# A hybrid decoder layer on one core: the passage from LayerNorm 1 to the seven-product FFN stage, with residual rows, evictions and statistics at other places in the queues

## The chip, the cores and the metric

The kernel runs on one core of a Trainium2 chip. The metric is the device time of one execution in microseconds (us). Engines are named as the profile names them: PE (matrix products) with PEld (its weight loads), DVE (vector), ACT (scalar activations), POOL, and SP, which issues most loads. Each engine takes its instructions in the order in which the program issues them, and waits at the first whose inputs, or whose output buffer, are not there yet.

## What is computed

One layer of a decoder for 512 prompt tokens and 32 sample tokens (8 sequences of 4), with model width 1024 and FFN width 2816, all in float32. Cut to the part around the change:

```
x = layer_norm(ALPHA * x + (1 + g1) * y, ln1_g, ln1_b)      # y: the merged branches times w_out
u = x * (1 + sc2) + sh2
h = (silu(u @ w_gate) * (u @ w_up)) @ w_down
x = layer_norm(ALPHA * x + (1 + g2) * h, ln2_g, ln2_b)
```

`sc2`, `sh2`, `g1`, `g2` come from a conditioning vector, one for the prompt and one for each sample sequence. Ahead of this lie one input projection, a causal convolution, dilated attention over prompt and caches, and their merge.

## The kernel before

**Halves and splits.** Activations lie transposed, with channels on the 128 partitions and the 544 tokens along the free axis, and are worked on in two halves of 272 tokens (`HC`), called half 0 and half 1. Every matrix operand is split into a high and a low part in a format that PE takes faster than full float32, and a product is three passes: high by high, high by low, low by high (lines 199, 200 and 202 in `mm_group`). A weight tile of 128 by 1024 is therefore split before use by `prep_to`: ACT casts it to the high part (line 133), DVE subtracts to get the low part (line 134). `w_next(look)` prepares up to `look` tiles ahead and returns the next one. There are four raw buffers (`wr`); a load into one is issued by SP (line 117) when the tile that lay in it has been split.

**Output projection and LayerNorm 1 (lines 977 to 1007).** For each half, eight output tiles m = 0 to 7 are computed (24 products each); DVE adds each into the residual `z` (line 991, in half 1 also 995 and 997), and `stats.feed(m)` collects LayerNorm statistics: a running sum `lns` on DVE (line 881) and a running sum of squares `lnq` (the square on ACT, line 873, the addition on POOL, line 882). After each tile `tick()` advances the background generators in `bg` by one step. When a half is done, `ln1_gen` is put in `bg` and advanced once: `stats.finish` adds the last tile (line 918) and yields. The next step has PE add up the sums over partitions (lines 922 and 923, against a matrix of ones), ACT and DVE make the reciprocal deviation (926 to 935), and the normalised rows are turned into the FFN input `u2[h]`: DVE multiplies (954), ACT scales and shifts (956) and casts to the high part (960), DVE subtracts to the low part (950). For half 0 this is spread over the steps by `LN1_CUTS`, and after one empty step four further steps of two rows each make two things for each row k on ACT: a copy of the FFN input in `TF` (line 974), which is needed later, and the residual row `z * ALPHA * g + ALPHA * b` in place (line 975), which nothing reads before the down projection. The steps that are still left when half 1 is done are run in `while bg: tick()`, ahead of the last addition of half 1.

**First FFN tiles (j = 0, lines 1223 to 1300).** `w_gu` holds gate and up tiles in turn, here called gu0, gu1, and so on; tiles 2f and 2f+1 belong to hidden tile f. Hidden tiles 0 and 1 (gu0 to gu3) are computed for half 0 first (`first`), with the statistics of half 1 between its second and third group on PE, and then for half 1 (`second`, lines 1259 to 1265, 96 products). Hidden tiles 2 and 3 are classical: gate product `pg` (48 products), up product `pu` (48), then `gu_evict`: two sigmoids on ACT (1015), the gate multiplied in and the up product multiplied in on DVE (1017, 1019), cast and low part of the result (1021, 1023). The products lie in four PSUM banks of the pool `pmm`, so `pg` of hidden tile 3 takes the banks of `pg` of hidden tile 2 and cannot start before these have been read. The sigmoid tiles `sgf` come from two buffers (tag `w`).

Between these products the operands of the next stage are made: sums and differences of the blocks of u2 (`tf`, `t3`, `t4`, lines 1252 to 1257), and their high and low parts S1, S2, S3 and A22 (1253, 1256, 1269, 1272, 1275, 1278, 1279, 1289). `keep(k)` does for half 1 what line 975 does for half 0. `add_up` (POOL, line 1071) makes sums of the raw blocks of the weights into `SS`, whose buffer is that of `t3`; `unit` splits such a block (ACT 1087, DVE 1098).

**Seven-product stage (`seven`, hidden tiles 4 to 20).** A hidden tile takes seven products of half size (lines 1114 to 1116) in place of eight. The order of the work on all engines is written out by hand: while PE works at tile f, ACT, DVE and POOL split and add up the blocks of tile f + 1, and what is left of tile f's eviction (`rest`: `c12`, `lo0`, `m1`, `hi1`, `lo1`) runs at the start of the next tile. For j = 0 the tiles are 4, 5, 6 and 7; `copies` after each issues copies of the caches from ACT's queue.

**What sets the order.** PE, ACT, DVE and POOL run exactly in program order. A buffer that is taken again waits for the last reader of the tile that lay in it.

Of the kernel before, what the change touches and what calls it, by code (L numbers as in the profile page):

```python
# [9 lines left out]
AF = mybir.ActivationFunctionType  # L10
# [6 lines left out]
NT = 544  # L17
# [37 lines left out]
def hybrid_step_kernel(ctx: ExitStack, tc: tile.TileContext, I, O):  # L55
# [37 lines left out]
    def big_tile(i, shape, dt, name):  # L93
        return big.tile(shape, dt, tag=f"L{i}", name=name)
# [45 lines left out]
    def w_next(look=PLOOK):  # L140
        i = pos["use"]
        prep_to(i + look)
        pos["use"] = i + 1
        return preps.pop(i)
# [718 lines left out]
    class Stats:  # L863
# [42 lines left out]

        def finish(self, tail, pairs=(0, 2)):
            if tail:
# [8 lines left out]
            else:  # L917
                self.add(7)
                yield
                pq = ps_t.tile([128, 512], F32, tag="t", name="lnps2")  # L920
                pd = ps_o.tile([128, 512], F32, tag="o", name="lnps")
# [18 lines left out]
    def f32(ap):  # L940
        return ap.bitcast(F32)

    def ln1_gen(h, stats):
        sd = yield from stats.finish(False, (0, 2) if h else ())
        A = big_tile(5 + h, [128, 2, 8, HC], F32R, f"u2{h}")
# [22 lines left out]
        if h == 0:  # L968
            yield
            for k in range(8):  # L970
                if k % 2 == 0:
                    yield
                zk = stats.zt(k)
                act.activation(out=TF[0][:, k // 4, k % 4], in_=zk, func=AF.Identity, scale=G9[:, k, 0:1], bias=B9[:, k, 0:1])
                act.activation(out=zk, in_=zk, func=AF.Identity, scale=agb[:, 0, k:k + 1], bias=agb[:, 1, k:k + 1])

# [32 lines left out]

    def gu_evict(pg, pu, Hs, fi):  # L1010
        hs = list(pg)
        sg = {}
        for h in hs:
            sg[h] = tmp.tile([128, HC], F32, tag="w", name="sgf")
            act.activation(out=sg[h], in_=pg[h][:, :HC], func=AF.Sigmoid)
        for h in hs:
            dve.tensor_tensor(out=sg[h], in0=sg[h], in1=pg[h][:, :HC], op=ALU.mult)  # L1017
        for h in hs:
            dve.tensor_tensor(out=sg[h], in0=sg[h], in1=pu[h][:, :HC], op=ALU.mult)
        for h in hs:  # L1020
            act.copy(out=Hs[h][:, 0, fi], in_=sg[h])
        for h in hs:
            dve.tensor_tensor(out=Hs[h][:, 1, fi], in0=sg[h], in1=Hs[h][:, 0, fi].bitcast(F32), op=ALU.subtract)

    def down_evict(ps, m, h):
# [81 lines left out]
    def unit(f, n):  # L1107
        unit_high(f, n)()
# [110 lines left out]
    for j, (k0, k1) in enumerate(FF_CHUNKS):  # L1219
# [3 lines left out]
        if j == 0:  # L1223
# [21 lines left out]

            def keep(k):
                zk = z[:, k, HC:NT]
                act.activation(out=zk, in_=zk, func=AF.Identity, scale=agb[:, 0, k:k + 1], bias=agb[:, 1, k:k + 1])

# [6 lines left out]
            act.copy(out=T["S2"][:, 0], in_=tf[:, 3])  # L1256
            dve.tensor_tensor(out=t4, in0=tf[:, 1], in1=tf[:, 3], op=ALU.subtract)
            A = u2[1]
            for k in range(8):
# [7 lines left out]
            for i in range(2):  # L1267
                gu_evict({1: second[2 * i]}, {1: second[2 * i + 1]}, H, i)
            dve.tensor_tensor(out=T["S1"][:, 1], in0=tf[:, 0], in1=f32(T["S1"][:, 0]), op=ALU.subtract)
            prep_to(pos["use"] + 2)  # L1270
            pu = mm_group(w_next(2), u2, 8)
            dve.tensor_tensor(out=T["S2"][:, 1], in0=tf[:, 3], in1=f32(T["S2"][:, 0]), op=ALU.subtract)
            TA = big_tile(0, [128, 2, 2, 4, HC], F32R, "ta")
            T["S3"], T["A22"] = TA[:, 0], TA[:, 1]
            act.copy(out=T["S3"][:, 0], in_=t3)
            keep(0)
            keep(1)
            dve.tensor_tensor(out=T["S3"][:, 1], in0=t3, in1=f32(T["S3"][:, 0]), op=ALU.subtract)
            act.copy(out=T["A22"][:, 0], in_=t4)
            keep(2)  # L1280
            keep(3)
            own["SS"] = one.tile([128, 3, 4, 128], F32, tag="vT", name="ss")
            gu_evict(pg, pu, H, 2)
            prep_to(pos["use"] + 2)
            f = 4
            for n in ("S1", "S2", "S3"):
                add_up(f, n)
            pg = mm_group(w_next(2), u2, 8)
            dve.tensor_tensor(out=T["A22"][:, 1], in0=t4, in1=f32(T["A22"][:, 0]), op=ALU.subtract)
            own["S4"] = one.tile([128, 2, 4, 128], F32R, tag="osb", name="s4")  # L1290
            for k in range(4, 8):
                keep(k)
            unit(f, "A11")
            unit(f, "S1")
            add_up(f, "S4")
            pu = mm_group(w_next(1), u2, 8)
            unit(f, "S2")
            gu_evict(pg, pu, H, 3)
            unit(f, "A12")
            rest["a22"] = unit_high(f, "A22")  # L1300
        for f in wg:
            hooks = {}
            if f == wg[-1]:
                u = pos["use"] + 2
                hooks = {2: lambda: prep_to(u + 1), 4: lambda: prep_to(u + 2)}
            seven(f, f - k0, H, f + 1 in wg, hooks)
            copies(0.8)
        ring.clear()
# [181 lines left out]
```

## Time and profile before

| | us |
|---|---|
| median of 3 runs | 1039.72 (1038.31 to 1041.39) |
| the profiled execution | 1039.63 |
| its span in the profile | 1037.9 |
| PE busy | 989.9 (95%) |
| DVE busy | 647.1 (62%) |
| ACT busy | 480.8 (46%) |
| POOL busy | 233.5 (23%) |

Times in the rows of the profile are us from the start of the span. A row of the timeline gives the start, the duration, the engine, the line of the kernel, the operation, output and inputs by the program's names with the shape, and the count if equal neighbours were merged (the start is then the first one's). A bracket at the end gives the idle time of the engine just before, and what released it. Matmuls are pipelined, so that one starts about 0.125 us after the other although each is shown with 0.29 us. A row of the table of windows gives, for each engine, busy time and number of instructions, then the clock that PE was granted (1.00 is full), then the share and the rate of the DMA engines.

### The profile page before, as it was taken

How to read it: one execution, taken by the hardware profiler on the slowest of the kernel's cores; microseconds unless marked ns; L12 is line 12 of the kernel's file. 1: busy time of each engine (PE TensorE's matmuls, PEld its weight loads, DVE VectorE, ACT ScalarE, POOL GpSimd, SP SyncE). 2: the span in 40 equal slices, each digit the busy share in tenths (PEclk: the TensorE clock that was granted, in tenths of full speed). 3: DMA queues.
4: the chain of work that ended last, by engine and by line, in shares of the span. 5: the costliest groups of instructions: out<-in, count | busy, mean ns of one | idle time of the engine just before them, and what ended most of it. 6: DMA issues, size and time to landing. Idle time of an engine off the chain costs nothing.

```text
span 1037.9 us, 21539 instructions
## 1 busy us (share of the span) xinstructions
PE 989.9 (95%) x8964; PEld 946.5 (91%) x8964; DVE 647.1 (62%) x1156; ACT 480.8 (46%) x931; POOL 233.5 (23%) x279
## 2 busy tenths in 40 slices
PE   4999999999999999999999997889999999999995
PEld 3987999999989989999999987889999999999994
DVE  3422788879886554343228876757636885478687
ACT  3312235545447666543434356556315552266333
POOL 0201010010014310101103534034014440354046
PEclk9999999999999999999999998989999999999998
DMA  9898687686785574799943620124964668665612
GB/s 379 362 387 316 236 301 273 246 330 239 281 302 196 205 264 161 264 373 393 361 165 105 246 63 21 48 67 171 345 243 173 259 216 325 235 247 202 217 51 86
DMA packets 44945, 242.64 MB, mean 234 GB/s; under 512 B 7408, under 2 KB 10736, under 8 KB 37680
## 3 DMA queue, kind: packets, MB, share of 16 engines
q1 hardware_dynamic: 34592, 126.83, 34.0%
q10 hardware_dynamic: 7632, 88.43, 22.7%
q0 software_dynamic: 2624, 26.02, 6.2%
q8 instruction: 70, 1.15, 0.4%
q14 instruction: 27, 0.22, 0.1%
HBM read 231.36 MB, written 97.58 MB: 317 GB/s over the span
## 4 chain that ended last, share of the span: by engine, by line
PE 65%; DVE 11%; issue 8%; ACT 7%; POOL 5%; DMA 4%; ACTq 0%; DVEq 0%; POOLq 0%
PE mm L199 16%; PE mm L200 15%; PE mm L202 15%; POOL ss L1071 3%; DMA wr<-in_w_gu 2%; PE mm L1114 2%; PE mm L1115 2%; PE mm L1116 2%; PE od L740 2%; PE Sd L705 2%; PE adaps L334 1%; PE pt L516 1%; DVE mrg L829 1%; DMA wr<-in_w_in 1%; DVE wl L134 1%
## 5 line engine op out<-in xcount | busy, mean ns | idle before, releaser
L199 PE MATMUL mm<-u,wh 128*128 128x272 f32 x1016 | 285.0, 298 | 6.4 <-DVE sgf L1017 6.4
L200 PE MATMUL mm<-u,wh 128*128 128x272 f32 x1016 | 277.0, 290 | 0.0
L202 PE MATMUL mm<-u,wl 128*128 128x272 f32 x1016 | 213.7, 290 | 0.5 <-DVE wl L134 0.5
L199 PEld LDWEIGHTS mm<-u,wh 128*128 128x128 f32 x1016 | 193.7, 191 | 20.9 <-issue 11.0
L200 PEld LDWEIGHTS mm<-u,wh 128*128 128x128 f32 x1016 | 193.9, 191 | 0.4
L134 DVE TENSOR_TENSOR wl<-wr,wh 128x1024 fp32r<-128x1024 f32 (+2 forms) x100 | 116.3, 1164 | 85.8 <-ACT wh L133 85.0
L202 PEld LDWEIGHTS mm<-u,wl 128*128 128x128 f32 x1016 | 161.3, 190 | 0.7 <-DVE wl L134 0.7
L133 ACT CAST wh<-wr 128x1024 fp32r<-128x1024 f32 (+2 forms) x100 | 97.0, 972 | 66.5 <-PE mm L200 50.5
L439 DVE SCALAR_TENSOR_TENSOR convy<-glu,vec,convy 128x512 f32<-128x512 f32 x120 | 95.6, 796 | 2.5
L1071 POOL TENSOR_TENSOR ss<-wr 128x512 f32<-128x512 f32 x34 | 50.2, 1476 | 189.0 <-DVE s L1098 90.2
L200 PE MATMUL mm<-h,wh 128*128 128x272 f32 x240 | 64.7, 288 | 0.0
L199 PE MATMUL mm<-h,wh 128*128 128x272 f32 x240 | 64.5, 286 | 0.0
L1028 DVE SCALAR_TENSOR_TENSOR z<-mm,modT,z 128x272 f32<-128x272 f32 (+1 forms) x48 | 21.6, 478 | 51.2 <-PE mm L202 51.2
L637 ACT ACTIVATE qk<-mm,vec 128x272 f32<-128x272 f32 (+1 forms) x48 | 25.9, 627 | 56.5 <-PE mm L202 56.5
L202 PE MATMUL mm<-h,wl 128*128 128x272 f32 x240 | 49.6, 288 | 0.0
L1087 ACT CAST wh<-ss 128x512 fp32r<-128x512 f32 (+1 forms) x34 | 28.4, 835 | 43.6 <-POOL ss L1071 30.6
L199 PEld LDWEIGHTS mm<-h,wh 128*128 128x128 f32 x240 | 45.2, 188 | 0.0
L200 PEld LDWEIGHTS mm<-h,wh 128*128 128x128 f32 x240 | 45.1, 188 | 0.0
L509 ACT ACTIVATE P<-P,st 128x256 f32<-128x256 f32 x64 | 31.2, 489 | 28.3 <-DVE st L503 25.8
L654 POOL DMA_DIRECT2D out_kv<-qk x4 | 2.4, 599 | 182.5 <-ACT qk L637 182.5
L1114 PE MATMUL mm<-ta,wh 128*128 128x272 f32 x136 | 40.4, 297 | 0.9 <-DVE wg L1136 0.8
L200 PE MATMUL mm<-mrg,wo 128*128 128x272 f32 x128 | 37.9, 296 | 1.8 <-DVE mrg L829 1.7
(330 smaller groups left out, 2544.6 us busy)
## 6 DMA issues: line engine op xcount, KB each, us to landing
out_s<-in_c ACTq DMA_DIRECT2D x32, 2044.0 KB, 9.7
wr<-in_w_in SPq DMA_DIRECT2D x60, 512.0 KB, 6.5
wr<-in_w_gu SPq DMA_DIRECT2D x44, 512.0 KB, 4.1
KT<-in_kt SPq DMA_DIRECT2D x24, 792.0 KB, 8.0
VV<-in_vv SPq DMA_DIRECT2D x24, 768.0 KB, 7.4
gb<-in_w_ada POOLq DMA_DIRECT2D x8, 2048.0 KB, 16.6
out_s<-in_c ACTq DMA_DIRECT2D x8, 2032.0 KB, 10.5
ga<-in_w_ada SPq DMA_DIRECT2D x8, 1024.0 KB, 14.4
```

Of the source, the lines that this page charges most:

```text
L133: act.copy(out=hv, in_=raw)
L134: dve.tensor_tensor(out=lv, in0=raw, in1=hv.bitcast(F32), op=ALU.subtract)
L199: pe.matmul(ps[h][:, :HC], lhsT=hi[:, k], rhs=A[h][:, 0, k], start=(k == 0), stop=False)
L200: pe.matmul(ps[h][:, :HC], lhsT=hi[:, k], rhs=A[h][:, 1, k], start=False, stop=False)
L202: pe.matmul(ps[h][:, :HC], lhsT=lo[:, k], rhs=A[h][:, 0, k], start=False, stop=(k == nk - 1))
L439: dve.scalar_tensor_tensor(out=o, in0=src, scalar=sc, in1=o, op0=ALU.mult, op1=ALU.add)
L509: act.activation(out=p[:, a:b], in_=p[:, a:b], func=AF.Exp, bias=st[:, kd, s, hh, 0:1], accum_out=st[:, kd, s, hh, 1:2])
L637: act.activation(out=o, in_=src, func=AF.Identity, bias=V("b_in", col))
L1028: dve.scalar_tensor_tensor(out=zz[:, :n1], in0=ps[:, :n1], scalar=modT[:, 5, m, 0:1], in1=zz[:, :n1], op0=ALU.mult, op1=ALU.add)
L1071: pool.tensor_tensor(out=o, in0=x, in1=y, op=op)
L1087: act.copy(out=hi, in_=src_of(f, n))
L1114: pe.matmul(ps[:, :HC], lhsT=hi[:, k], rhs=B[:, 0, k], start=(first and k == 0), stop=False, skip_group_check=not first)
```

## The change

Three things are changed, none of which changes what is computed:

1. **LN1's first statistics one output tile later.** `finish` gets an argument `late`; for half 0 it yields a second time between the last addition and the products with `ones`. All later steps of half 0's `ln1_gen` thereby come one output tile of half 1 later.
2. **Residual rows put off.** Line 975 is gone from `ln1_gen`. `keep` now takes a count and works through 16 rows, half 0 first: four after the block differences, two after the low part of S2, two after the low part of A22, and two behind each of the four seven-product tiles of j = 0. Before, the eight rows of half 1 were four around S3 and A22 and four after the low part of A22.
3. **Classical evictions split in two.** `gu_evict` is divided into `gate_evict` (sigmoids and gate multiplication) and `up_evict` (the rest). For hidden tiles 2 and 3 the gate part is issued ahead of the up product's weights and products. With it the low parts of S1 and S2 move behind the issue of hidden tile 2's up product, S3 behind its eviction, the split of gu7 behind the three `add_up`, and in hidden tile 3 the blocks A11 and S1 of the weights ahead of the gate eviction, the high part of A22 and the S4 sum behind it.

```diff
-        def finish(self, tail, pairs=(0, 2)):
+        def finish(self, tail, pairs=(0, 2), late=False):
...
                 self.add(7)
                 yield
+                if late:
+                    yield
...
-        sd = yield from stats.finish(False, (0, 2) if h else ())
+        sd = yield from stats.finish(False, (0, 2) if h else (), h == 0)
...
-                act.activation(out=zk, in_=zk, func=AF.Identity, scale=agb[:, 0, k:k + 1], bias=agb[:, 1, k:k + 1])
...
+    def gate_evict(pg):
+        sg = {}
+        for h in pg:
+            sg[h] = tmp.tile([128, HC], F32, tag="w", name="sgf")
+            act.activation(out=sg[h], in_=pg[h][:, :HC], func=AF.Sigmoid)
+        for h in pg:
+            dve.tensor_tensor(out=sg[h], in0=sg[h], in1=pg[h][:, :HC], op=ALU.mult)
+        return sg
+
+    def up_evict(sg, pu, Hs, fi):
+        for h in sg:
+            dve.tensor_tensor(out=sg[h], in0=sg[h], in1=pu[h][:, :HC], op=ALU.mult)
+        for h in sg:
+            act.copy(out=Hs[h][:, 0, fi], in_=sg[h])
+        for h in sg:
+            dve.tensor_tensor(out=Hs[h][:, 1, fi], in0=sg[h], in1=Hs[h][:, 0, fi].bitcast(F32), op=ALU.subtract)
+
+    def gu_evict(pg, pu, Hs, fi):
+        up_evict(gate_evict(pg), pu, Hs, fi)
...
-            def keep(k):
-                zk = z[:, k, HC:NT]
-                act.activation(out=zk, in_=zk, func=AF.Identity, scale=agb[:, 0, k:k + 1], bias=agb[:, 1, k:k + 1])
+            keeps = [(k, h) for h in range(2) for k in range(8)]
+
+            def keep(n):
+                for _ in range(min(n, len(keeps))):
+                    k, h = keeps.pop(0)
+                    zk = z[:, k, h * HC:(h + 1) * HC]
+                    act.activation(out=zk, in_=zk, func=AF.Identity, scale=agb[:, 0, k:k + 1], bias=agb[:, 1, k:k + 1])
...
             dve.tensor_tensor(out=t4, in0=tf[:, 1], in1=tf[:, 3], op=ALU.subtract)
+            keep(4)
...
             pg = mm_group(w_next(2), u2, 8)
             for i in range(2):
                 gu_evict({1: second[2 * i]}, {1: second[2 * i + 1]}, H, i)
-            dve.tensor_tensor(out=T["S1"][:, 1], in0=tf[:, 0], in1=f32(T["S1"][:, 0]), op=ALU.subtract)
+            sg = gate_evict(pg)
             prep_to(pos["use"] + 2)
             pu = mm_group(w_next(2), u2, 8)
+            dve.tensor_tensor(out=T["S1"][:, 1], in0=tf[:, 0], in1=f32(T["S1"][:, 0]), op=ALU.subtract)
             dve.tensor_tensor(out=T["S2"][:, 1], in0=tf[:, 3], in1=f32(T["S2"][:, 0]), op=ALU.subtract)
+            keep(2)
+            up_evict(sg, pu, H, 2)
             TA = big_tile(0, [128, 2, 2, 4, HC], F32R, "ta")
             T["S3"], T["A22"] = TA[:, 0], TA[:, 1]
             act.copy(out=T["S3"][:, 0], in_=t3)
-            keep(0)
-            keep(1)
             dve.tensor_tensor(out=T["S3"][:, 1], in0=t3, in1=f32(T["S3"][:, 0]), op=ALU.subtract)
-            act.copy(out=T["A22"][:, 0], in_=t4)
-            keep(2)
-            keep(3)
             own["SS"] = one.tile([128, 3, 4, 128], F32, tag="vT", name="ss")
-            gu_evict(pg, pu, H, 2)
-            prep_to(pos["use"] + 2)
             f = 4
             for n in ("S1", "S2", "S3"):
                 add_up(f, n)
+            prep_to(pos["use"] + 2)
             pg = mm_group(w_next(2), u2, 8)
+            unit(f, "A11")
+            unit(f, "S1")
+            sg = gate_evict(pg)
+            act.copy(out=T["A22"][:, 0], in_=t4)
+            add_up(f, "S4")
             dve.tensor_tensor(out=T["A22"][:, 1], in0=t4, in1=f32(T["A22"][:, 0]), op=ALU.subtract)
             own["S4"] = one.tile([128, 2, 4, 128], F32R, tag="osb", name="s4")
-            for k in range(4, 8):
-                keep(k)
-            unit(f, "A11")
-            unit(f, "S1")
-            add_up(f, "S4")
+            keep(2)
             pu = mm_group(w_next(1), u2, 8)
             unit(f, "S2")
-            gu_evict(pg, pu, H, 3)
+            up_evict(sg, pu, H, 3)
...
             seven(f, f - k0, H, f + 1 in wg, hooks)
+            if j == 0:
+                keep(2)
             copies(0.8)
```

More of the change, by code (lines that the diff above doesn't have):

```diff
@@ L1007, in hybrid_step_kernel @@
         tick()
-    def gu_evict(pg, pu, Hs, fi):
-        hs = list(pg)
+    def gate_evict(pg):
         sg = {}
-        for h in hs:
+        for h in pg:
             sg[h] = tmp.tile([128, HC], F32, tag="w", name="sgf")
             act.activation(out=sg[h], in_=pg[h][:, :HC], func=AF.Sigmoid)
-        for h in hs:
+        for h in pg:
             dve.tensor_tensor(out=sg[h], in0=sg[h], in1=pg[h][:, :HC], op=ALU.mult)
-        for h in hs:
+        return sg
+    def up_evict(sg, pu, Hs, fi):
+        for h in sg:
             dve.tensor_tensor(out=sg[h], in0=sg[h], in1=pu[h][:, :HC], op=ALU.mult)
-        for h in hs:
+        for h in sg:
             act.copy(out=Hs[h][:, 0, fi], in_=sg[h])
-        for h in hs:
+        for h in sg:
             dve.tensor_tensor(out=Hs[h][:, 1, fi], in0=sg[h], in1=Hs[h][:, 0, fi].bitcast(F32), op=ALU.subtract)
+    def gu_evict(pg, pu, Hs, fi):
+        up_evict(gate_evict(pg), pu, Hs, fi)
     def down_evict(ps, m, h):
```

## Prediction

> **What bounds the kernel now.** I read the page first, its span and its busy shares.
>
> ```profile
> span 1037.9 us, 21539 instructions
> PE 989.9 (95%) x8964; PEld 946.5 (91%) x8964; DVE 647.1 (62%) x1156; ACT 480.8 (46%) x931; POOL 233.5 (23%) x279
> ```
>
> PE is the bound, and outside the stretch that is changed nothing moves. So what counts is where PE stands still between LN1 and the first seven-product tile: the timeline of PE alone, from 570 to 713 us, for its rows with a wait and for a few marks of place.
>
> ```profile
> 574.26 0.39 PE L200 MATMUL mm<-mrg,wo 128*128 128x272 f32 x1 [1.71 <-DVE mrg L829]
> ...
> 603.98 0.70 PE L922 MATMUL lnps<-lns,ones 128*128 128x272 f32 x2 [2.33 <-DVE lns L881]
> ...
> 638.86 1.28 PE L923 MATMUL lnps<-lnq,ones 128*128 128x272 f32 x2 [5.25 <-POOL lnq L882]
> ...
> 647.45 0.29 PE L1263 MATMUL mm<-u,wh 128*128 128x272 f32 x1
> ...
> 665.51 0.29 PE L199 MATMUL mm<-u,wh 128*128 128x272 f32 x1
> ...
> 666.64 0.52 PE L202 MATMUL mm<-u,wl 128*128 128x272 f32 x2 [0.47 <-DVE wl L134]
> ...
> 678.79 0.59 PE L199 MATMUL mm<-u,wh 128*128 128x272 f32 x1 [6.35 <-DVE sgf L1017]
> ...
> 693.34 0.29 PE L1114 MATMUL mm<-u,wh 128*128 128x272 f32 x1
> ...
> 712.25 0.39 PE L1114 MATMUL mm<-ta,wh 128*128 128x272 f32 x1 [0.24 <-DVE wg L1136]
> ```
>
> Four waits lie in the stretch: 2.33 + 5.25 + 0.47 + 6.35 = 14.4 us. Two of them cost more than their length, as the clock column of the windows shows:
>
> ```profile
> 575.00:576.00 1.00, 1.00 (x4) 1.00 (x5) 0.76 (x2) 0.17 (x1) 0.00 (x0) 0.50 0.98 386
> ...
> 604.00:610.00 6.00, 6.00 (x44) 5.84 (x45) 3.63 (x6) 2.49 (x4) 4.52 (x7) 1.00 0.35 110
> ...
> 643.00:644.00 1.00, 1.00 (x9) 1.00 (x8) 1.00 (x1) 0.00 (x0) 0.87 (x2) 0.89 0.04 16
> 684.00:685.00 1.00, 1.00 (x9) 1.00 (x9) 1.00 (x2) 0.24 (x1) 0.00 (x0) 0.91 0.83 311
> ```
>
> After the wait at 638.86 PE is back at full clock only about 643.2 (0.89 in its window), after that at 678.79 only about 684.2 (0.91). At half clock that loses 4.3/2 = 2.2 and 5.4/2 = 2.7 us. After the 2.33 us wait the clock stayed at 1.00, yet after one of 1.71 us (574.26) it fell to 0.50: what decides is not the length alone.
>
> **Part 1, LN1's sums.** The wait of 2.33 us goes: PE does tile 1 of half 1 first (24 products), and the last addition of half 0 is done by then. What comes late instead is read from DVE.
>
> ```profile
> 607.27 1.85 DVE L935 RECIPROCAL lnsd<-lnsd 128x272 f32<-128x272 f32 x1 [1.57 <-ACT lnsd L929]
> ...
> 612.67 0.46 DVE L991 SCALAR_TENSOR_TENSOR z<-mm,modT,z 128x240 f32<-128x240 f32 x1
> ...
> 613.91 0.79 DVE L954 TENSOR_TENSOR z<-z,lnsd 128x272 f32<-128x272 f32 x2
> ...
> 629.53 0.19 DVE L997 TENSOR_TENSOR z<-z,zsa 128x32 f32<-128x32 f32 x1
> ...
> 632.38 0.44 DVE L881 TENSOR_TENSOR lns<-lns,z 128x272 f32<-128x272 f32 x1
> ...
> 640.25 0.44 DVE L928 SCALAR_TENSOR_TENSOR lnsd<-lnps,lnsd 128x272 f32<-128x272 f32 x1 [0.15 <-PE lnps L923]
> ...
> 646.03 0.44 DVE L950 TENSOR_TENSOR u<-tf,u 128x272 fp32r<-128x272 f32 x1 [0.92 <-ACT u L960]
> ```
>
> DVE is nearly full here, so it and not PE paces half 1. Tile 1's residual and first sum (612.67 to 613.91, 1.24 us) now run before the reciprocal, in time that DVE spent waiting; the sums themselves come about 0.5 us later (PE ends tile 1 near 604.5, against 603.98). Net, the rest of DVE's row runs 0.7 us earlier: residual row 6 is ready at 629.72 - 0.7 = 629.0, the last addition at 632.1. A wait is added: half 1's first sum takes the buffer of half 0's and waits for PE's product; behind it stands only L928, which needs that product too, so I put it at zero (bounds 0 and 0.4). PE's full wait for a free bank, one tile later, I put at zero as well, since DVE paces.
>
> **Part 2, residual rows out of LN1.** The 5.25 us wait is for the squares of half 1, and its cause stands in ACT's row:
>
> ```profile
> 632.25 0.74 ACT L873 ACTIVATE lnsq<-z 128x272 f32<-128x272 f32 x2
> 632.89 0.60 ACT L974 ACTIVATE tf<-z,B,G 128x272 f32<-128x272 f32 x1
> ...
> 637.49 0.41 ACT L873 ACTIVATE lnsq<-z 128x272 f32<-128x272 f32 x1
> ```
>
> ```profile
> 638.04 0.76 POOL L882 TENSOR_TENSOR lnq<-lnq,lnsq 128x272 f32<-128x272 f32 x1 [3.64 <-ACT lnsq L873]
> ```
>
> Between the squares of rows 5, 6 and the last one stand eight instructions (four copies, four residual rows) in 4.6 us. After the change the residual rows are gone, but part 1 has pushed two more copies into this place, so six stand there. Independent rows take 0.53 us each (below, 2.13 for four). ACT is no longer behind, so it starts when row 6 is ready: 629.0 + 0.5 + 6 x 0.52 = 632.6 for the last square. POOL and PE follow 638.86 - 637.49 = 1.37 later: the product on the squares starts at 634.0, **4.9 us earlier**. PE, 2.3 earlier than before, still stands there for some 2.7 us in two pieces, for the sum and for the squares. Next on DVE's way to L928 stand gu3's cast and subtraction, queued behind the last square: 632.6 + 0.3 + 1.04 + 1.23 (durations of such a cast and subtraction below) = 635.2, against 640.25. So the chain of half 1 moves by 5.1 us, u2's first slice from 646.47 to 641.4.
>
> PE's second part starts with it, at 641.15 in place of 647.45 (its own work would let it start about 640.3 at full clock). From there 144 products to the up product of hidden tile 2 took 665.51 - 647.45 = 18.06, so it arrives at 659.2.
>
> **Part 3, four rows ahead of gu5.**
>
> ```profile
> 654.13 1.28 ACT L1015 ACT_TABLE_LOAD   x1
> ...
> 663.27 1.11 ACT L1256 CAST tb<-tf 128x1088 fp32r<-128x1088 f32 x1 [1.42 <-DVE tf L1255]
> 664.29 1.04 ACT L133 CAST wh<-wr 128x1024 fp32r<-128x1024 f32 x1
> ...
> 673.85 1.10 ACT L1275 CAST ta<-t 128x1088 fp32r<-128x1088 f32 x1 [3.15 <-DVE tb L1272]
> ...
> 676.87 1.12 ACT L1248 ACTIVATE z<-z,agb 128x272 f32<-128x272 f32 x2
> 677.88 0.66 ACT L1015 ACTIVATE sgf<-mm 128x272 f32<-128x272 f32 x2
> ...
> 681.08 2.13 ACT L1248 ACTIVATE z<-z,agb 128x272 f32<-128x272 f32 x4
> ```
>
> `keep(4)` stands right ahead of gu5's cast, with nothing to hide it: 664.29 - 5.1 + 2.1 = 661.3, done 662.3; the low part follows as before and PE's L202 stands at 666.64 - 5.1 + 2.1 = 663.6. So the wait of 0.47 grows to 3.1 for the high part plus 0.8 for the low part. Everything behind moves by only 3.0 us: the up product ends at 669.4, the evictions of `second` at 670.2 - 3.0 = 667.2.
>
> **Part 4, the split evictions.** The 6.35 us wait is for the gate multiplication of hidden tile 2, which stood behind S1, S2, S3, A22, four residual rows and the up product.
>
> ```profile
> 669.78 0.44 DVE L1023 TENSOR_TENSOR h<-sgf,h 128x272 fp32r<-128x272 f32 x1 [0.49 <-ACT h L1021]
> ...
> 674.98 1.29 DVE L1278 TENSOR_TENSOR ta<-t,ta 128x1088 fp32r<-128x1088 f32 x1 [1.22 <-ACT ta L1275]
> ...
> 681.21 1.23 DVE L134 TENSOR_TENSOR wl<-wr,wh 128x1024 fp32r<-128x1024 f32 x1 [0.35 <-ACT wh L133]
> ```
>
> Now it comes behind `second`. Its second sigmoid waits for the buffer freed at 667.2 (an added wait; queued behind it is gu6's cast); 0.4 and 0.5 later the bank is free, 668.2. gu6: cast 667.6 to 668.6, low part to 669.9. PE arrives at 669.3, so at most 0.2 is left of 6.35. Next is gu7, now behind more: S1 and S2 low (2 x 1.29) to 672.3, the up multiplications to 673.0, S3 high from 673.4, its low part to 675.8 (1.13 + 1.29 later, as at 673.85 and 674.98), then gu7's low part to 677.0. PE has done the gate product at 675.5 and the first four up products at 676.0, and waits 1.0 (bounds 0 and 2). The up product ends 5.8 later, 682.8, against 693.34: **10.5 us earlier**. The weight sums on POOL start at 675.9 and end near 681, before the stage needs them; the gate sigmoids, now waiting for PE ahead of A22, two rows and S2, find it done at 675.5.
>
> Against this stands the clock. A wait of 3.1 plus 0.8 within 4.4 us is between those that kept it and those that did not, and the 1.71 row says that it may well fall. Then the up product runs some 3.6 us at half clock and ends 1.8 later, but gu6 and gu7 are then no longer waited for (1.2), so 0.6 is left. I take it in. The Trainium skill, "TensorE: Matmul & The Clock Gate", has in its closing table that no idle gap above about 3 us should be left, and in Part 1 that the clock drops after one idle window of about 3.4 us. By it the waits of about 1 us cost nothing and this one stands at its edge; the row at 574.26 differs, it fell after 1.71. With no fall the sum would be 0.6 better.
>
> **Part 5, two rows behind each seven-product tile.** They stand on ACT ahead of the sigmoid of `c12` and of the split of S4.
>
> ```profile
> 706.09 0.40 ACT L1200 ACTIVATE wg<-c 128x272 f32<-128x272 f32 x1 [0.23 <-issue]
> ```
>
> ```profile
> 711.16 0.69 DVE L1098 TENSOR_TENSOR wl<-ss,hip 128x512 fp32r<-128x512 f32 x1 [1.09 <-POOL ss L1071]
> 711.76 0.43 DVE L1136 TENSOR_TENSOR wg<-wg,mm 128x272 f32<-128x272 f32 x1
> ```
>
> The split of S4 frees the buffer for POOL's next sum, whose split (711.16) stands on DVE ahead of U3 (711.76), and PE's product at 712.25 already waits 0.24 for U3. This loop has no slack: 1.05 us less the slack of 0.3 around L1200 (0.23 of it issue) is about 0.75 at PE in tile 5, and again in tile 6. Tile 7 has no next tile in this stage, tile 4 has nothing ahead of it: **1.5 us lost** (bounds 0 and 4 x 1.05 = 4.2).
>
> **Sum.** -10.5 + 0.6 + 1.5 = -8.4. The profiled execution took 1039.63, 1.7 beyond its span, and stands within 0.1 of the median, so 1039.7 - 8.4 = 1031.3 us.
>
> **Rivals.** *The four pairs are dearer*: if the loop does not catch up anywhere, they cost 4.2, and the sum is -5.7: 1034.0. For it speaks the 0.24 wait; against it that tile 7 lacks the split ahead of U3. *The pairs hide and the clock holds*: -10.5, 1029.2; for it speaks only that ACT is 46% busy. *The late sums gain nothing*: DVE ends half 1 where it did, the squares come 0.7 later and everything behind with them, 1032.0. *Slower, by table loads*: if the residual rows and the sigmoids do not share ACT's table, each of the seven places of `keep` costs two loads of 1.28 (654.13), 2.56 us. With six of them on the path and 1.5 of slack that is 13.9, and 1039.7 - 8.4 + 13.9 = 1045.2; it decides once loads stand at five places. Against it: the rows at 676.87 and 677.88 follow each other without one. *The change does not act*: if something else still stands in front of the gate multiplication, the 6.35 us stay with their cold clock, and only the 3.0 of part 3 less the 1.5 of part 5 is left: 1038.2. Against it: the two banks have no other reader.
>
> **Numbers.** The forecast 0.60, dearer pairs 0.15, hidden pairs 0.12, no gain from the late sums 0.07, table loads 0.03, no action 0.03. A measurement of this kernel tells a change from none beyond some 0.3%, 3.1 us. The first four are faster by more than that; no action mostly within it; so faster 0.93, same 0.03, slower 0.04. Range 1028.5 to 1034.5: from the hidden pairs, a little better, to the dear pairs.
>
> **What would show it.** Right: no wait for `lns` near 604; the product on the squares near 634; a wait of about 3 us at the up product of hidden tile 2, released by gu5 on ACT; less than 0.5 left at the next gate product; the first seven-product tile near 683; U3 waits of 0.7 to 1 us in tiles 5 and 6. Wrong: a table load between the rows, a wait above 2 us for gu7 or the weight sums, or a DVE that ends half 1 after 633.

## The result, and the profile after

The changed kernel took 1033.32 us, median of 4 runs (1032.24 to 1033.62); the kernel before, on the same chip, 1039.05, median of 4 (1038.31 to 1041.39). The ratio is 0.994, 95% interval 0.9927 to 0.9954: faster by 5.7 us, where 8.4 was forecast. The profiled execution took 1033.35 with a span of 1031.6, 6.3 less than before. Of all runs in this document one, the fourth of e7_no_pair_mid, was slow (1600.63 us at a granted clock of 0.557), and it is left out below.

The page of the kernel after: its span and busy time of each engine.

```profile
span 1031.6 us, 21539 instructions
PE 985.8 (96%) x8964; PEld 942.2 (91%) x8964; DVE 652.1 (63%) x1156; ACT 479.7 (47%) x931; POOL 236.3 (23%) x279
```

The work is the same to the instruction. But DVE became busier by 5.0 us and POOL by 2.8, with no instruction more: the same operations took longer. That is a first sign of the step that failed. It is a rough one: in a second profile of this kernel (e11_again, below) the rises are 2.6 and 1.7, and of the 5.0 here 3.4 belong to the four subtractions treated below.

The timeline of PE in the kernel after, from LN1 to the third seven-product tile: the rows that answer to those of before.

```profile
632.39 0.72 PE L924 MATMUL lnps<-lns,ones 128*128 128x272 f32 x2 [1.72 <-DVE lns L881]
634.65 1.27 PE L925 MATMUL lnps<-lnq,ones 128*128 128x272 f32 x2 [1.54 <-POOL lnq L882]
...
644.03 0.29 PE L1274 MATMUL mm<-u,wh 128*128 128x272 f32 x1
...
663.19 0.39 PE L199 MATMUL mm<-u,wh 128*128 128x272 f32 x1 [0.93 <-ACT wh L133]
...
664.45 0.52 PE L202 MATMUL mm<-u,wl 128*128 128x272 f32 x2 [0.49 <-DVE wl L134]
...
677.80 0.52 PE L202 MATMUL mm<-u,wl 128*128 128x272 f32 x2 [0.73 <-DVE wl L134]
...
683.41 0.29 PE L1120 MATMUL mm<-u,wh 128*128 128x272 f32 x1
...
693.33 0.39 PE L1120 MATMUL mm<-ta,wh 128*128 128x272 f32 x1 [2.18 <-DVE wg L1142]
...
705.06 0.39 PE L1120 MATMUL mm<-ta,wh 128*128 128x272 f32 x1 [0.88 <-DVE wg L1142]
...
716.80 0.39 PE L1120 MATMUL mm<-ta,wh 128*128 128x272 f32 x1 [0.90 <-DVE wg L1142]
```

Read it from the end. Tile 4 starts at 683.41, 9.9 us earlier than before (693.34). The 6.35 us wait at the gate product is gone; in its place 0.73 is left for gu7. From there on some of the gain is given back: 2.18 us in tile 4, where before listed no wait, 0.88 in tile 5 (0.24 before), and 0.90 in tile 6. So 9.9 - 2.2 - 0.6 - 0.9 = 6.2, against 6.3 between the spans. The gain was made as forecast, and lost in three waits for U3.

### The profile page after: what moved, and what is told of

It is laid out like the page before. It is cut to its first block, busy times and chain, and to the rows that moved or that the text cites. A ratio compares the mean times of both kernels' runs of the same rounds, so it can differ in the third digit from the quotient of the medians.

```text
span 1031.6 us, 21539 instructions
## 1 busy us (share of the span) xinstructions
PE 985.8 (96%) x8964; PEld 942.2 (91%) x8964; DVE 652.1 (63%) x1156; ACT 479.7 (47%) x931; POOL 236.3 (23%) x279
## 4 chain that ended last, share of the span: by engine, by line
PE 61%; DVE 12%; issue 8%; ACT 7%; POOL 6%; DMA 5%; ACTq 0%; DVEq 0%; POOLq 0%
PE mm L199 15%; PE mm L200 14%; PE mm L202 14%; POOL ss L1077 4%; DMA wr<-in_w_gu 3%; PE od L740 2%; PE mm L1120 2%; PE Sd L705 2%; PE mm L1121 2%; PE mm L1122 2%; PE adaps L334 1%; DVE mrg L829 1%; DMA wr<-in_w_in 1%; PE pt L516 1%; DVE wl L134 1%
## 5 line engine op out<-in xcount | busy, mean ns | idle before, releaser
L202 PE MATMUL mm<-u,wl 128*128 128x272 f32 x1016 | 213.2, 290 | 1.3 <-DVE wl L134 1.2
L202 PEld LDWEIGHTS mm<-u,wl 128*128 128x128 f32 x1016 | 160.4, 189 | 1.9 <-DVE wl L134 1.9
L202 PE MATMUL mm<-h,wl 128*128 128x272 f32 x240 | 49.6, 288 | 0.0
```

What stands on the lines that cost most here:

```text
L202: pe.matmul(ps[h][:, :HC], lhsT=lo[:, k], rhs=A[h][:, 0, k], start=False, stop=(k == nk - 1))
```

## The experiments

Each kernel is the changed kernel with the edit shown. The changed kernel itself was run once more with the last group, under the label e11_again, as a measure of what two sets of runs differ by:

> The changed kernel once more, beside the two runs that are built on it: 1033.3, as before, with a wait of 2.2 us for U3 in tile 4 and 0.9 in tiles 5 and 6. No theory expects anything else.

It took 1032.28 (1032.11 to 1033.26, 5 runs; ratio 0.9936, 0.9924 to 0.9949), 1.0 less than the first median. So a difference of 1 us between two kernels below tells nothing. PE's timeline of this execution, tiles 4 and 6 (tile 5 has no such wait):

```profile
692.28 0.39 PE L1120 MATMUL mm<-ta,wh 128*128 128x272 f32 x1 [2.18 <-DVE wg L1142]
...
715.77 0.40 PE L1120 MATMUL mm<-ta,wh 128*128 128x272 f32 x1 [0.52 <-DVE wg L1142]
```

The wait of tile 4 is as expected, those of tiles 5 and 6 are not (0 and 0.52 for 0.9 each). After tile 4's wait the granted clock fell to 0.50 here (window 694 to 697), where the first profile has 1.00, so PE came later to the next products and waited less. The time is the same: from the row of tile 4 to that of tile 6 it is 23.49 us here and 23.47 in the first profile. So waits of single products may be compared only between executions whose clock was the same there.

**First statistics put off: undone (e1_no_late).**

```diff
-        sd = yield from stats.finish(False, (0, 2) if h else (), h == 0)
+        sd = yield from stats.finish(False, (0, 2) if h else ())
```

> Part 1 undone alone: half 0's sums go back to one output tile earlier. Theory (DVE and ACT set when the product on the squares of half 1 can start, PE only waits there): PE stands 2.3 us near 604 again, but only four copies instead of six are left ahead of the last square, so that product starts near 633.8 in place of 634.65 and everything behind it is 0.5 to 0.9 us earlier than in the changed kernel: about 1032.5. PE's wait at the sums of half 1 is then under 1 us and its clock does not fall there. Rival (the 2.33 us were a gain of their own): the time goes up by 2.3 us, about 1035.6.

Measured: 1032.56 (1031.84 to 1034.22, 5 runs; ratio 0.9936, 0.9924 to 0.9949). Two rows of PE's timeline of this kernel:

```profile
603.87 0.70 PE L924 MATMUL lnps<-lns,ones 128*128 128x272 f32 x2 [2.33 <-DVE lns L881]
...
633.17 0.73 PE L924 MATMUL lnps<-lns,ones 128*128 128x272 f32 x2 [0.31 <-DVE lns L881]
```

The 2.33 us wait is back, and PE comes to the second sum that much later, so that it waits 0.31 there instead of 1.72, and not at all for the squares behind it. The wait only changes its place, since DVE and ACT pace half 1 of LN1. This part of the change is worth nothing that these runs can tell; the rival that it brings 2 us or more falls.

**Residual rows of half 0 back in LN1 (e2_rows_in_ln1).**

```diff
+                act.activation(out=zk, in_=zk, func=AF.Identity, scale=agb[:, 0, k:k + 1], bias=agb[:, 1, k:k + 1])
...
-            keeps = [(k, h) for h in range(2) for k in range(8)]
+            keeps = [(k, 1) for k in range(8)]
```

> Part 2 undone for half 0: its eight residual rows stand in LN1 again, so none is left behind the seven-product tiles; half 1's eight rows take the first places (four, two, two). Theory: twelve instructions in place of six ahead of the last square, so the product on the squares starts near 638.5, 3.9 us later, and the up product of hidden tile 2 and the first seven-product tile are later by as much; tiles 5 and 6 get back 1.5. Net 2.4 slower than the changed kernel, about 1035.7. Rival (PE's own work is the bound from there on, since its clock fell there anyway): first seven-product tile at most 1 us later and the time the same or better, 1032 to 1033.

Measured: 1035.8 (7 runs; ratio 0.9971, 0.996 to 0.9982), some 3 us slower than the changed kernel. PE's timeline of this kernel has the long wait for the squares again:

```profile
637.46 1.27 PE L925 MATMUL lnps<-lnq,ones 128*128 128x272 f32 x2 [5.41 <-POOL lnq L882]
```

The wait of tile 4 (at 696.13) stays at 2.18, to the hundredth. So it does not come from the eight rows moved here; those of half 1 are still in the passage and are treated below (e7, e4). Tiles 5 and 6 have no wait, but the clock fell to 0.58 ahead of them (697 to 700), so that this alone doesn't show what the rows cost there.

**Evictions whole, in the old order (e3_no_split).**

```diff
-            sg = gate_evict(pg)
+            dve.tensor_tensor(out=T["S1"][:, 1], in0=tf[:, 0], in1=f32(T["S1"][:, 0]), op=ALU.subtract)
...
-            keep(2)
-            up_evict(sg, pu, H, 2)
...
+            act.copy(out=T["A22"][:, 0], in_=t4)
...
+            gu_evict(pg, pu, H, 2)
+            prep_to(pos["use"] + 2)
...
-            up_evict(sg, pu, H, 3)
+            gu_evict(pg, pu, H, 3)
```

> Part 4 undone: from the gate product of hidden tile 2 on the order of the kernel before, the gate multiplication behind S1, S2, S3, A22 and the up product; rows where they are now (four ahead of gu5, two behind each of the four tiles), the other four after A22's low part. Theory: the wait for the bank comes back with some 5 us, the clock falls and loses 2 us more, but POOL's sums then run while DVE waits and tile 4 loses its 2.2 us wait. First seven-product tile 6 to 7 us later, net 4 slower: about 1037. Rival (parts 1 and 2 alone made the gain): within 1 us of the changed kernel.

Measured: 1036.02 (1035.02 to 1037.71, 11 runs; ratio 0.9968, 0.9959 to 0.9976). PE's timeline of this kernel:

```profile
676.08 0.44 PE L199 MATMUL mm<-u,wh 128*128 128x272 f32 x1 [4.34 <-DVE sgf L1017]
```

The gate product waits 4.34 us again, and the wait in tile 4 is gone: the four POOL sums take 1.28 to 1.48 here and DVE's subtractions 0.68 to 1.28, the durations of the kernel before. So the split, with the order that belongs to it, is worth about 3 us (4 were expected), and it is what brings tile 4's wait.

**Two theories of tile 4's wait.** The rows of DVE in the kernel after, as the split leaves them:

```profile
676.53 1.22 DVE L134 TENSOR_TENSOR wl<-wr,wh 128x1024 fp32r<-128x1024 f32 x1
677.66 1.78 DVE L1104 TENSOR_TENSOR wl<-wr,wh 128x512 fp32r<-128x512 f32 x1
679.58 1.57 DVE L1104 TENSOR_TENSOR wl<-ss,wh 128x512 fp32r<-128x512 f32 x1
681.07 0.77 DVE L1017 TENSOR_TENSOR sgf<-sgf,mm 128x272 f32<-128x272 f32 x2
681.76 1.68 DVE L1302 TENSOR_TENSOR ta<-t,ta 128x1088 fp32r<-128x1088 f32 x1
683.42 2.27 DVE L1104 TENSOR_TENSOR wl<-ss,wh 128x1024 fp32r<-128x1024 f32 x1
685.61 0.77 DVE L1022 TENSOR_TENSOR sgf<-sgf,mm 128x272 f32<-128x272 f32 x2
...
688.43 0.69 DVE L1104 TENSOR_TENSOR s<-ss,s 128x512 fp32r<-128x512 f32 x1 [0.34 <-ACT s L1093]
...
692.24 0.69 DVE L1104 TENSOR_TENSOR wl<-ss,hip 128x512 fp32r<-128x512 f32 x1 [1.36 <-POOL ss L1077]
692.85 0.43 DVE L1142 TENSOR_TENSOR wg<-wg,mm 128x272 f32<-128x272 f32 x1
```

And those of POOL:

```profile
676.69 2.20 POOL L1077 TENSOR_TENSOR ss<-wr 128x512 f32<-128x512 f32 x1 [28.19 <-DVE ta L1290]
678.97 1.63 POOL L1077 TENSOR_TENSOR ss<-ss,wr 128x512 f32<-128x512 f32 x1
680.56 1.74 POOL L1077 TENSOR_TENSOR ss<-wr 128x512 f32<-128x512 f32 x1
682.26 2.34 POOL L1077 TENSOR_TENSOR ss<-wr,ss 128x512 f32<-128x512 f32 x1
```

The same four subtractions and the first of the same sums in the kernel before, DVE first, then POOL (the other three sums took 1.27 to 1.29):

```profile
682.35 1.28 DVE L1289 TENSOR_TENSOR ta<-t,ta 128x1088 fp32r<-128x1088 f32 x1
683.75 0.69 DVE L1098 TENSOR_TENSOR wl<-wr,wh 128x512 fp32r<-128x512 f32 x1
684.37 0.68 DVE L1098 TENSOR_TENSOR wl<-ss,wh 128x512 fp32r<-128x512 f32 x1
688.42 1.23 DVE L1098 TENSOR_TENSOR wl<-ss,wh 128x1024 fp32r<-128x1024 f32 x1 [3.38 <-ACT wh L1087]
```

```profile
676.35 1.27 POOL L1071 TENSOR_TENSOR ss<-wr 128x512 f32<-128x512 f32 x1 [23.64 <-DVE ta L1278]
```

Before, POOL's first three sums ran while DVE mostly stood; now they lie beside DVE's subtractions, and both are slower. The four subtractions take 1.78 + 1.57 + 1.68 + 2.27 = 7.3 us in place of 3.9. The multiplications that read a PSUM bank (0.77 for two, at 681.07) are not slower beside the same sums.

The rows say more than that both are slower: the two engines take turns. The subtraction at 676.53 began first, kept its 1.22 us and ended at 677.75. POOL's sum beside it ended 1.14 later (678.89), DVE's next subtraction 0.55 after that (679.44), POOL's next sum 1.16 after that (680.60), and so on down to 685.69. Each step is 0.11 to 0.14 less than what the same instruction takes alone (1.27 for a sum, 0.69 for a subtraction of 128x512). So what the stretch costs can be added up from durations measured alone, by taking the instructions of both engines one after the other.

Everything behind the four subtractions on DVE is late: the up eviction starts at 685.61, 2.0 us after PE has finished, then the low part of S4 (688.43) frees the buffer for POOL's next sum (689.20), whose split (692.24) stands ahead of U3 (692.85). My theory was this sharing between DVE and POOL. (S4's own sum is not waited for: it ended at 684.60, and ACT's cast of it began at 687.78 without a wait.) The rival: DVE's and ACT's casts stand still because they wait for POOL's sums, and the lengths matter little.

**Splits that don't read POOL's sums (e5_units_raw), and one sum in place of four (e6_one_sum).** In e5 the splits of S1 and S2 of tile 4 read the raw blocks, POOL still makes all sums; in e6, on top of the edit of e5, it makes only that of S4 in tile 4.

```diff
+        if f == 4 and n in ("S1", "S2"):
+            return {"S1": u[:, 0:4], "S2": u[:, 0:8]}[n]
```

```diff
-        pool.tensor_tensor(out=o, in0=x, in1=y, op=op)
+        if f == 4 and n == "S4":
+            y = u[:, 0:4]
+        if f != 4 or n == "S4":
+            pool.tensor_tensor(out=o, in0=x, in1=y, op=op)
```

> In hidden tile 4 the weight blocks S1 and S2 are split from the raw tiles in place of POOL's sums (other numbers, same sizes); POOL makes the same four sums at the same time, but nobody waits for the first three. Theory (POOL's sums slow DVE's subtractions by sharing something, no one waits for their result): DVE's four subtractions beside them stay at 1.6 to 2.3 us in place of 0.69 to 1.28, the U3 wait in tile 4 stays at 1.5 to 2.2, time as the changed kernel, about 1033. Rival (ACT and DVE wait for late sums): the U3 wait in tile 4 falls under 0.5 and the time by 2.

> As the run with raw blocks, and POOL makes one of the four sums only (the last, from raw blocks), so three of them are left out. Theory (sharing): DVE's subtractions of tile 4 are back at 0.7, 0.7, 1.3 and 1.2 us, but for the one beside the sum; the up eviction of hidden tile 3 starts within 0.3 of the end of its products, the U3 wait in tile 4 falls to 0.3 or less, the waits of 0.9 in tiles 5 and 6 stay; 2 us faster than the changed kernel, about 1031. Rival (order of ACT's or DVE's queue): the U3 wait stays near 2 although the subtractions are short.

Measured: e5 1032.7 (1032.15 to 1033.53, 4 runs; ratio 0.9936, 0.9922 to 0.9949), e6 1030.67 (1030.18 to 1031.32, 4 runs; ratio 0.9914, 0.9899 to 0.993). PE's timeline of e5:

```profile
692.15 0.39 PE L1122 MATMUL mm<-ta,wh 128*128 128x272 f32 x1 [2.17 <-DVE wg L1144]
```

DVE's timeline of e6 over the same operations:

```profile
677.57 2.39 DVE L1109 TENSOR_TENSOR wl<-wr,wh 128x512 fp32r<-128x512 f32 x2
...
680.58 1.28 DVE L1307 TENSOR_TENSOR ta<-t,ta 128x1088 fp32r<-128x1088 f32 x1
681.78 1.21 DVE L1109 TENSOR_TENSOR wl<-wr,wh 128x1024 fp32r<-128x1024 f32 x1
```

With nobody waiting for the first sums the wait stays at 2.17; with the sums gone it goes, and the two subtractions that have no sum beside them fall back from 1.68 and 2.27 to 1.28 and 1.21. That settles it: the wait of tile 4 comes from the sharing. The rival falls.

**No pair of rows ahead of the cast of S2 (e7_no_pair_mid).**

```diff
-            keep(2)
             pu = mm_group(w_next(1), u2, 8)
...
             flush()
+            if j == 0:
+                keep(2)
```

> The two residual rows ahead of S2's cast in hidden tile 3 taken away from there; two rows more at the start of the first down projection. Theory (sharing on DVE): S2's cast waits for POOL's sum in place of the rows, the U3 wait in tile 4 stays at 1.8 or more, time as the changed kernel within 0.5. Rival (ACT's queue, these rows): the U3 wait in tile 4 falls by 1 us or more and so does the time.

Measured: 1034.7, median of three runs (1033.38 to 1034.81; ratio 0.995, 0.9935 to 0.9966). The change was expected to stay within 0.5 of the changed kernel; the ratios differ by some 1 us, which tells nothing. The wait of tile 4 is 2.17 still. That these rows in ACT's queue are behind it falls too.

**U3 ahead of the low part of S1 and the sum of S4 (e8_u3_first).** If DVE is late, it should at least do first what PE waits for.

```diff
         tt(U2, s1, Y, ALU.add)
-        if nxt:
-            lo()
-            add_up(f + 1, "S4")
...
         tt(U3, U2, Zc, ALU.add)
         tt(C22, U3, Zd, ALU.add)
         if nxt:
+            lo()
+            add_up(f + 1, "S4")
             unit(f + 1, "S2")
```

> In every seven-product tile the low part of the next tile's S1 and POOL's S4 sum are issued behind U3 and C22 in place of ahead of U2's successor. Theory (the loop over S4, POOL and S1 reaches PE only through U3's place behind S1's low part in DVE's queue): the waits of 2.2, 0.9 and 0.9 in tiles 4, 5 and 6 go to 0.2 or less, and the small ones of later tiles with them: 3.5 to 4.5 faster than the changed kernel, 1029 to 1030. Rival (U3 is late by itself, or the delay comes back one product later through S4's sum): 1 us or less.

Measured: 1033.21 (1032.23 to 1034.85, 5 runs; ratio 0.994, 0.9927 to 0.9952), no better than the changed kernel: a miss. PE's timeline of this kernel, tiles 4 to 7:

```profile
690.57 0.40 PE L1120 MATMUL mm<-ta,wh 128*128 128x272 f32 x1 [0.31 <-DVE wg L1142]
...
702.60 0.39 PE L1120 MATMUL mm<-ta,wh 128*128 128x272 f32 x1 [0.96 <-DVE wg L1142]
...
714.34 0.40 PE L1120 MATMUL mm<-ta,wh 128*128 128x272 f32 x1 [0.90 <-DVE wg L1142]
...
726.28 0.39 PE L1120 MATMUL mm<-ta,wh 128*128 128x272 f32 x1 [1.09 <-DVE wg L1142]
```

Tile 4's wait falls from 2.18 to 0.31, but those of tiles 5 and 6 stay, and tile 7, which had none, gets 1.09. So the waits of tiles 5 and 6 do not come through POOL's buffer, or not by it alone. DVE's timeline of e8 after a pair of residual rows:

```profile
698.45 0.44 DVE L1142 TENSOR_TENSOR wg<-wg,c 128x272 f32<-128x272 f32 x1 [0.86 <-ACT wg L1205]
```

DVE stands 0.86 us for the sigmoid of `c12`, which stands on ACT behind the pair of rows. Behind that multiplication are the low parts and U2 and U3 (701.57), one queue without gaps. That is a second way from the rows to PE, about as late as the first.

**No rows in the passage and stage (e4_rows_in_down), and that with U3 first (e10_rows_u3).** All 16 residual rows go into the first down loop, two ahead of each eviction that uses them:

```diff
-            keeps = [(k, h) for h in range(2) for k in range(8)]
+            keeps = [(k, h) for k in range(8) for h in range(2)]
...
-            keep(4)
...
                 ps = mm_group(w_next(), H, nf)
+                if j == 0:
+                    keep(2)
                 for h in range(2):
                     down_evict(ps[h], m, h)
```

with the other calls of `keep` gone. e10 has the edit of e8 as well.

> All sixteen residual rows moved into the first down projection, two ahead of the eviction that reads them; none in the passage or behind the tiles. Theory (rows cost what they hold up on ACT): the wait at gu5 shrinks from 1.42 to 0.5 or less, the one at gu7 goes, the U3 waits in tiles 5 and 6 fall from 0.9 to 0.24 or less, the one in tile 4 stays mostly (1.5 to 2.2, POOL's sums slow DVE). Together 3 us faster than the changed kernel: about 1030.3. Rival (the U3 waits are not from the rows): tiles 5 and 6 still wait 0.9 and the gain is 1 us at most.

> Residual rows in the first down projection and U3 ahead of S1's low part, statistics one tile later as in the changed kernel. Theory (U3 first gave nothing because the rows lengthen the loop over the sigmoid of c12, m1, A11's low part and U2 to 11.7 us a tile, so that what tile 4 saved was waited off in tiles 5 to 7): with the rows gone the saving stays. Tile 4 waits 0.4 or less in place of 2.2, tiles 5 to 7 not at all; 1.8 us faster than with the rows moved alone, about 1027.9. Rival (the loop is as long without the rows, DVE's queue is full): tiles 5 to 7 wait 0.5 or more and the time is that of the rows moved alone, 1029.7.

Measured: e4 1029.72 (1029.65 to 1030.82, 4 runs; ratio 0.991, 0.9897 to 0.9922), e10 1027.97 (1027.69 to 1028.73, 4 runs; ratio 0.9895, 0.9881 to 0.9908). In PE's timeline of e4 the wait at gu5 is gone, the one at gu7 stays at 0.73 against what was expected, the wait of tile 4 stays, and those of tiles 5 and 6 are gone (in the down loop, where the rows now stand, PE has no wait of 0.12 or more from 725 to 770):

```profile
690.37 0.39 PE L1120 MATMUL mm<-ta,wh 128*128 128x272 f32 x1 [2.17 <-DVE wg L1142]
```

PE's timeline of e10, tiles 4 and 5 (tile 6 has no wait, tile 7 one of 0.39):

```profile
688.65 0.39 PE L1120 MATMUL mm<-ta,wh 128*128 128x272 f32 x1 [0.33 <-DVE wg L1142]
...
700.00 0.39 PE L1120 MATMUL mm<-ta,wh 128*128 128x272 f32 x1 [0.29 <-DVE wg L1142]
```

The changed kernel, e4, e8 and e10 are the four cases of rows and order. Tile 4's wait follows the order alone (2.18 and 2.17 against 0.31 and 0.33). For tiles 5 and 6 the fair pair is e8 and e10, where the clock was 1.00 from 676 to 735: 0.96 and 0.90 with the rows, 0.29 and none without. (In e4 the clock fell to 0.50 after tile 4's wait, window 691 to 694, which may hide a wait in tile 5.) Tile 7's wait comes with the new order, 1.09 with the rows and 0.39 without. What the rows do shows best in the pace of the loop, whatever the clock did: DVE's multiplication by the sigmoid of `c12` comes every 11.74 to 11.76 us from tile 4 to tile 6 in the two profiles of the changed kernel and in e8, and every 10.81 to 11.04 in e4 and e10. Both edits together take away nearly all. e10 beats both kernels: 11.0 us under the kernel before, 4.3 under the lower median of the changed one.

**e10 with the first statistics where they were (e9_best).** The edit of e1 on top of e10.

> As the run before, and half 0's sums not put off. Theory: the product on the squares of half 1 starts 0.8 us earlier as in the run without that part, and nothing holds this up behind: 1027.2. Rival (with the rows gone PE's own work is the bound there, and the 2.3 us wait near 604 returns): 1 to 2 us slower than with the sums put off, 1029 to 1030.

Measured: 1028.16 (1027.95 to 1028.67, 4 runs; ratio 0.9897, 0.9882 to 0.9912). That putting them off costs 0.8, as e1 seemed to say, falls, and so does the rival's 1 to 2 us the other way: the two can't be told apart.

## Why the prediction was right, and where it failed

The sign, the range and the mechanism of the gain were right: 1033.3 in 1028.5 to 1034.5. Against the forecast of -8.4 the span shows -6.3, the medians -5.7.

*LN1.* No wait near 604, as said. The product on the squares stood at 634.65, for 634.0. The last square began at 633.28, 0.7 later than worked out, and PE followed 1.37 behind it, as worked out. DVE's row of the kernel after says where the time went:

```profile
626.77 2.29 DVE L881 TENSOR_TENSOR lns<-lns,z 128x272 f32<-128x272 f32 x3
```

Three additions took 2.29 us. In the kernel before, three took 1.38 and, a moment later, two took 1.94. That is the same sharing, and the trace of before had it in two rows:

```profile
627.58 1.38 DVE L881 TENSOR_TENSOR lns<-lns,z 128x272 f32<-128x272 f32 x3
...
629.64 1.94 DVE L881 TENSOR_TENSOR lns<-lns,z 128x272 f32<-128x272 f32 x2
```

```profile
626.84 0.77 POOL L899 TENSOR_TENSOR lnq<-lnq,lnsq 128x272 f32<-128x272 f32 x1 [15.06 <-ACT lnsq L873]
629.53 2.69 POOL L882 TENSOR_TENSOR lnq<-lnq,lnsq 128x272 f32<-128x272 f32 x3 [1.92 <-ACT lnsq L873]
```

The pair at 629.64 has POOL's additions beside it (629.53), the three at 627.58 have not. The prediction read only the rows that carried its sum, and took each duration from where it happened to stand.

*gu5.* The wait was 0.93 + 0.49, for 3.1 + 0.8. PE's second part started at 644.03, not 641.15, for it came out of LN1 at half clock (next point); it arrived at 662.26 in place of 659.2, and the four rows were nearly over. L202 stood at 664.45, for 663.6: ACT's row decides this point whenever PE arrives, and its cast, worked out for 661.3, began at 662.11. Where the clock didn't fall in LN1, the forecast wait came: in e5, e6 and e7, whose work up to here is that of the changed kernel, PE stood 2.79 to 2.80 us for gu5's high part.

*The clock.* The forecast had it fall at gu5 and lose 0.6. In this execution it fell at LN1's squares, before gu5. The windows of the kernel after:

```profile
632.00:635.00 3.00, 1.07 (x3) 0.65 (x4) 0.67 (x2) 3.00 (x7) 0.76 (x1) 0.83 0.00 0
635.00:638.00 3.00, 3.00 (x13) 2.76 (x13) 2.85 (x4) 0.73 (x2) 2.71 (x3) 0.50 0.38 60
638.00:641.00 3.00, 3.00 (x15) 3.00 (x15) 2.88 (x4) 0.40 (x1) 1.97 (x3) 0.53 0.31 120
```

After two waits of 1.72 and 1.54 the granted clock was 0.50 to 0.53 for about six microseconds; after 0.93 and 0.49 at gu5 it stayed at 1.00 (window 664 to 667). After the same two waits in LN1 (1.71 or 1.72, and 1.53) it stayed at 1.00 in e5, e6 and e7, and fell at gu5 there, as forecast. What PE lost in LN1 it would have stood at gu5 otherwise, so it cost little: the product behind gu5's wait stood at 663.19 here and at 663.26 in e7. Tile 4 began at 683.41, against 682.8 + 0.6. That these agree to the hundredth is luck: the 0.6 was not lost to the clock at gu5; gu5's low part came 0.85 late, mainly since LN1's squares did, and gu7 took 0.27 less than the 1.0 put in.

*The split evictions.* The 6.35 us went and gu7 left 0.73 (bounds 0 to 2, 1.0 taken). That part of the sum was right.

*The step that failed.* This is the term that the sum put at nothing: "The weight sums on POOL start at 675.9 and end near 681, before the stage needs them", and with it "tile 4 has nothing ahead of it". They started at 676.69 and ended at 684.6, and the subtractions of DVE beside them took 3.4 us longer. Tile 4 lost 2.18 for a term that the sum did not have. e5, e6 and e3 show it: the wait stays when nobody reads the sums, goes when they are not made, and goes when the subtractions run at another time. The Trainium skill, "GPSIMD Engine Reference", section "Specifications", states that GpSimd's SBUF interfaces are shared with VectorE, with contention for VectorE instructions that have two SBUF inputs. The trace agrees, down to the exception: the subtractions with two SBUF inputs went from 0.69 to 1.57 and 1.78, the multiplications with one input in PSUM stayed at 0.77 for two. These rows also show how: of two such instructions, the one that begins second waits for the first to end.

*The pairs of rows.* 0.88 - 0.24 and 0.90 were lost in tiles 5 and 6, for 0.75 each: 1.5 in all, as forecast. The path given was only half of it. The prediction saw the split of S4, POOL's buffer and the split of S1; e8 cut that path and the waits stayed. The sigmoid of `c12` and DVE's queue behind it are as late, and e10 against e8, with the pace of the loop in e4, shows that the rows are the cause. Which of the two paths binds in the changed kernel is not shown.

*The rivals.* Dearer pairs (1034.0) came nearest to the first median, but for another reason: the pairs cost what was said, and tile 4's wait came from POOL. The second median, 1032.28, lies nearest to late sums that gain nothing (1032.0). There is no table load between the rows and the sigmoids, and the split did act. That the late sums gain nothing was right as to the part itself (e1, e9); the forecast had 0.7 us on it.

What the two sets of runs of the changed kernel differ by, 1.0 us, is not settled; the last section shows one thing that can do it, the clock at 574.

## What to carry to other kernels

When a step is moved, look at what the engine that shares its memory path does at the new time: DVE and POOL side by side on operands in SBUF took turns here, so that the durations of both have to be added (7.3 us in place of 3.9 for DVE's four subtractions). More busy time for the same count of instructions on the page is a hint of it, though it moved by 2.4 us between two executions of one kernel; the durations of the rows decide. A reordering that takes away a wait is best costed through to the next two waits behind it, by all queues that the late instruction stands in, not by the first path that explains a row. Small work that no one needs soon (here 16 rows of 0.5 us) belongs ahead of its use in a stage with slack, and not in a loop that has none: that gave some 3 us more, and the order of one queue in favour of PE a further 1.8.

## What the runs showed of the hardware

**DVE and POOL wait for each other.** A subtraction of 128x512 from SBUF took 0.69 us alone and 1.57 to 1.78 beside a POOL sum, one of 128x1024 1.23 and 2.27; POOL's sum of 128x512 took 1.27 alone and 1.63 to 2.34. Each ended 0.11 to 0.14 us less than its own time alone after the other engine's instruction had ended; the first of the chain kept its 1.22.

**The clock's answer to a wait differs from one execution to the next.** The same product in the second profile of the changed kernel (e11_again), in PE's timeline, with its wait (1.73 at 574.19 in the first profile, 1.71 at 574.26 in the kernel before):

```profile
574.18 0.39 PE L200 MATMUL mm<-mrg,wo 128*128 128x272 f32 x1 [1.72 <-DVE mrg L829]
```

Its window from 577 to 578 us, and behind it that of the first profile:

```profile
577.00:578.00 1.00, 1.00 (x10) 1.00 (x9) 0.85 (x1) 1.00 (x3) 0.00 (x0) 1.00 1.03 409
```

```profile
577.00:578.00 1.00, 1.00 (x6) 1.00 (x6) 0.84 (x1) 1.00 (x3) 0.11 (x1) 0.50 1.03 392
```

The clock was 1.00 in the one and 0.50 in the other, after waits of 1.72 and 1.73 in the same kernel. PE did 10 products against 6 in that microsecond, and from LN1 on the rows of the execution that kept its clock stand about 1 us earlier (spans 1030.5 and 1031.6). Likewise it stayed at 1.00 after 2.33 us in e1, and was 0.58 from 605 to 608 after 3.06 us in e9; and after tile 4's wait of 2.18 it stayed in the first profile of the changed kernel and fell in the second. The Trainium skill, "TensorE: Matmul & The Clock Gate", has in Part 1 that the window in which activity is counted runs free, so that the same kernel differs from run to run; these two executions agree. Its closing table asks for no idle gap above some 3 us; here a gap of 1.73 was enough for the clock to fall. So the length of a wait alone does not tell what it costs, and a term of 1 us for a clock that may fall belongs in the range, not in the sum.
